# Cosine-similarity attention on one core: a third polynomial chunk, statistics instructions for Q, and one normalisation for two heads

## The chip, the cores and the metric

The kernel runs on one core of a Trainium2 chip. A core has five engines that matter here, each with an instruction queue of its own that is worked off strictly in order: TensorE (PE, matrix multiply; PEld is its weight load), VectorE (DVE), ScalarE (ACT), GpSimd (POOL) and SyncE (SP, which issues most DMAs). An instruction that waits for a semaphore holds everything behind it on its engine. The metric is the device time of one execution in microseconds; the kernel before has a median of 189.31 us over three runs (189.05 to 189.56).

## The reference, cut to what matters

```python
Q_norm = Q / (np.linalg.norm(Q, axis=-1, keepdims=True) + 1e-10)     # batch 8, heads 12, seq 512, dim 64
K_norm = K / (np.linalg.norm(K, axis=-1, keepdims=True) + 1e-10)
scores = np.einsum('bhqd,bhkd->bhqk', Q_norm, K_norm) / tau          # tau = 0.1
weights = np.exp(scores - np.max(scores, axis=-1, keepdims=True))
weights = weights / (np.sum(weights, axis=-1, keepdims=True) + 1e-10)
return np.einsum('bhqk,bhkd->bhqd', weights, V)
```

There are 96 heads. Each needs the norms of 512 rows of Q and of K, a 512 x 512 matrix of scores, 262,144 exponentials, and a product with V. Scores lie between -10 and 10, so the kernel leaves the maximum out.

## The kernel before, in words

**Tiling.** Two heads make a pair, 48 pairs in all, and a pair is one turn of a software pipeline. A pair's scores are made transposed, keys on the partitions: four chunks of 128 keys, each with 512 queries of both heads, so a chunk is a tile of 128 x 1024. Chunks alternate between two halves of a four-bank PSUM tile `scps`. The score of chunk n+2 can start when the exponential of chunk n has been read out, and that handover between TensorE and ScalarE is the innermost loop of the kernel.

**Stages of a pair.**

1. SP loads Q and K (tile `qk`, a ring of 15 pairs) and V (tile `vf`, a ring of 10).
2. GpSimd squares Q and K in one instruction (`sq`, line 366). TensorE adds the squares up with an identity matrix: 16 matmuls for Q and K together (line 396, pairs in `SUM_BOTH`), into a spare corner of the bank in which the output is summed. VectorE reduces the rest (line 410). Four pairs (35, 39, 43, 47, `BY_VECTOR`) are reduced by VectorE from the squares alone (line 418).
3. VectorE finds 1/norm for a group of one, two or four pairs at a time with a bit trick and two rounds of polynomial steps (lines 441 to 473, small tiles). The first three pairs use ScalarE's Ln and Exp for it.
4. Q is scaled by VectorE and K by VectorE or GpSimd (line 485; `K_ON_DVE` lists the pairs whose K goes to VectorE, 20 of 48).
5. TensorE transposes Q and K (line 494, 8 matmuls), VectorE evacuates the result (line 512, "the evacuation", tile `qt`).
6. TensorE makes the scores (line 633), ScalarE the exponentials (line 657, tile `et`).
7. GpSimd casts V to bf16 with a column of ones beside it (line 665, tile `vb`), so that the product also gives the sum of the weights. TensorE multiplies (line 682, 32 matmuls of 65 columns a pair) into two banks `oops`, one for each head.
8. VectorE takes the reciprocal of the sum (line 701) and multiplies (line 703), once for each head. SP stores the pair (line 707).

**Chunks that ScalarE does not do.** Chunk 3 of pairs 36 and 45 (`OFF`) gets its exponentials another way: scores go to the bank of the transposes (line 568), VectorE splits them into a power of two and a remainder (lines 573 and 575, for each head), and GpSimd evaluates a polynomial of the remainder in six steps (lines 596 to 604).

**What sets the order.** Nothing is decided at run time. Every operation is added to a list (`P.add`) with the operations it needs; `ORDER` then gives, for each engine, the written-out sequence of list numbers. `run` turns needs into semaphore waits. On each engine an operation thus waits for its own needs and for all that stands before it.

Of the kernel before, what the change touches and what calls it, by code (L numbers as in the profile page):

```python
# [108 lines left out]
def bass_cosine_similarity_attention_kernel(  # L109
# [70 lines left out]

    def key(name, s, *rest):
        return (name, s) + rest if s >= 0 else None
# [8 lines left out]
        vb[:, :, :, :, DIM : DIM + 1].rearrange("p r c h o -> p (r c h o)"), 1.0))  # L191
# [131 lines left out]
    def pair(s):  # L323
# [210 lines left out]
    def last_step(s, c):  # L534
        return 5 if (s, c) in OFF_ON_POOL + OFF_ON_BOTH else 4

# [17 lines left out]
    def poly(s, c, at):  # L554
# [4 lines left out]
        a0, a1, a2, a3, a4 = POLY_K if here else POLY  # L559
# [39 lines left out]
        if (s, c) in OFF_ON_POOL:  # L599
            k = cc ** 0.5  # L600
            steps = [("pool", "yt", mul(w, z, z)), ("pool", "ys", add(w, w, a1, k)),
                     ("pool", "ys", lambda e: e.tensor_scalar(out=z, in0=z, scalar1=a2 * cc, scalar2=a3 * cc, op0=ALU.mult, op1=ALU.add)),
                     ("pool", "yt", mul(w, w, w)), ("pool", "yt2", lambda e: e.tensor_tensor(out=w, in0=w, in1=z, op=ALU.add)),
                     ("pool", "yt3", mul(e_, w, p2))]
        elif (s, c) in OFF_ON_BOTH:
# [13 lines left out]
    def rest(s):  # L619
# [41 lines left out]
        def cast(e):  # L661
            out = vb[:, iq, :, :, 0:DIM].rearrange("p c h d -> p h c d")
            in_ = vf[iv][:, :, :].rearrange("p h (c d) -> p h c d", c=NT)
            if not in_psum(s):
                return e.tensor_scalar(out=out, in0=in_, scalar1=1.0, scalar2=1.0, op0=ALU.mult, op1=ALU.mult)  # L665
            assert s + R_QK >= NP and off_of[s] == NT - 1
            e.tensor_scalar(out=out[:, :, 0 : NT - 1], in0=in_[:, :, 0 : NT - 1], scalar1=1.0, scalar2=1.0, op0=ALU.mult, op1=ALU.mult)
            e.memset(vb[:, iq, NT - 1, :, DIM : DIM + 1].rearrange("p h o -> p (h o)"), KAPPA)
            return e.tensor_scalar(out=out[:, :, NT - 1], in0=in_[:, :, NT - 1], scalar1=KAPPA, scalar2=1.0, op0=ALU.mult, op1=ALU.mult)

        P.add(("VC", s), "pool", "vck" if in_psum(s) else "vc", T0 + 3.0 - slack(s, M_VC), [("LV", s), key("PV", s - R_QK, 0, NT - 1), key("PV", s - R_QK, 1, NT - 1), "vone"], cast)
# [3 lines left out]
        for h in range(2):  # L675
            for i in range(NT):
                def pv(e, h=h, i=i):
                    for c in range(NT):
                        t = i
                        if s in off_of:  # L680
# [28 lines left out]
    def last(s, T0):  # L709
        iq, iet, io = s % R_QK, s % R_ET, s % R_O  # L710
        spare = t_ps[:, :, :, :].rearrange("p w t x -> p (w t x)").bitcast(f32)
        for k, (h, lo, hi) in enumerate(PIECES):
            bank = spare if k == 2 else o_ps[h]
            order = [c for c in range(NT - 1) if c != off_of.get(s)] + [off_of[i] for i in (s,) if i in off_of] + [NT - 1]
            for j, c in enumerate(order):
                def pv(e, h=h, lo=lo, hi=hi, c=c, bank=bank, j=j):
                    for t in range(lo, hi):
                        at = 65 * (t - lo)
                        last = e.matmul(
                            out=bank[:, at : at + 65], lhsT=et[iet][:, c, h, 128 * t : 128 * t + 128],  # L720
                            rhs=vb[:, iq, c, h, :], start=(j == 0 and t == lo), stop=(j == NT - 1), skip_group_check=True)
# [3 lines left out]
                           [("EXP", s, c, k) if c == NT - 1 else exps(s, c)[0], ("VC", s)]  # L725
# [25 lines left out]
POLY = (-186.9751803485176, 100772.4799431421, -50373599.073513225, 207520169.07623482, 3.565140779347853e-11)  # L751
OFF = {(36, 3): (36, 36), (45, 3): (45, 45)}
# [14 lines left out]
STATS_FROM = 99  # L767
# [42 lines left out]
def slack(s, most):  # L810
# [129 lines left out]
```

## Time and profile before

| | us |
|---|---|
| median of three runs | 189.31 (189.05 to 189.56) |
| span of the profiled execution, first to last instruction | 186.8 |
| ScalarE busy | 180.2 |
| TensorE busy | 179.5 |
| GpSimd busy | 165.7 |
| VectorE busy | 159.9 |

The profile describes one execution, whose span is 186.8 us; what lies around the span (2.5 us up to the median) is not in it. A row of a group of instructions gives source line, engine, operation, the tiles written and read, their shapes, the count, busy time, mean duration in ns, and the idle time ahead of them with its releaser. A row of a timeline gives start, length, engine, line and a count where equal instructions were merged. Instructions of one engine overlap: the next starts before the last has drained, so the distance between two starts is what an instruction costs its engine, and its duration is longer. Lateness that is shorter than this overlap is not printed as idle time.

### The profile page before, as it was taken

How to read it: one execution, taken by the hardware profiler on the slowest of the kernel's cores; microseconds unless marked ns; L12 is line 12 of the kernel's file. 1: busy time of each engine (PE TensorE's matmuls, PEld its weight loads, DVE VectorE, ACT ScalarE, POOL GpSimd, SP SyncE). 2: the span in 40 equal slices, each digit the busy share in tenths (PEclk: the TensorE clock that was granted, in tenths of full speed). 3: DMA queues.
4: the chain of work that ended last, by engine and by line, in shares of the span. 5: the costliest groups of instructions: out<-in, count | busy, mean ns of one | idle time of the engine just before them, and what ended most of it. 6: DMA issues, size and time to landing. Idle time of an engine off the chain costs nothing.

```text
span 186.8 us, 7242 instructions
## 1 busy us (share of the span) xinstructions
PE 179.5 (96%) x3010; PEld 117.9 (63%) x3010; DVE 159.9 (86%) x523; ACT 180.2 (96%) x210; POOL 165.7 (89%) x147
## 2 busy tenths in 40 slices
PE   7889999999999999999999999999999999998993
PEld 2456766666667666666676666766656566555653
DVE  2789998987987978979889988999999999998664
ACT  5799999999999999999999999999999999999992
POOL 3799999999989998999999899999999999907940
PEclk9999999999999999999999999999999999999999
DMA  5999999999999877999999999999798731113135
GB/s 158 354 349 351 349 358 329 288 351 364 370 376 369 283 245 230 309 303 307 312 379 367 328 371 335 319 312 298 241 303 294 239 105 56 60 56 116 60 112 168
DMA packets 52447, 50.79 MB, mean 272 GB/s; under 512 B 3136, under 2 KB 52416, under 8 KB 52416
## 3 DMA queue, kind: packets, MB, share of 16 engines
q1 hardware_dynamic: 51984, 50.02, 81.8%
q8 instruction: 23, 0.38, 0.8%
q10 hardware_dynamic: 432, 0.33, 0.5%
q14 instruction: 8, 0.07, 0.1%
HBM read 37.75 MB, written 12.58 MB: 269 GB/s over the span
## 4 chain that ended last, share of the span: by engine, by line
ACT 92%; PE 3%; DVE 2%; DMA 1%; POOL 0%; issue 0%; DVEq 0%
ACT et L657 91%; DMA qk<-in_K_dram 1%; PE oops L682 1%; PE scps L633 1%; DVE xs L260 1%; DVE ob L732 0%; POOL sq L256 0%; PE tps L283 0%; ACT ys L432 0%; DVE qn L273 0%; DVE ob L703 0%; PE oops L401 0%; ACT nps L435 0%; PE oops L281 0%; DVE rd L730 0%
## 5 line engine op out<-in xcount | busy, mean ns | idle before, releaser
L657 ACT ACTIVATE et<-scps 128x1024 bf16<-128x1024 f32 (+1 forms) x191 | 173.8, 1155 | 0.3 <-PE scps L633 0.3
L366 POOL TENSOR_TENSOR sq<-qk 128x1024 bf16<-128x1024 f32 x44 | 82.8, 1895 | 0.6 <-DMA qk<-in_K_dram 0.6
L633 PE MATMUL scps<-qt 64*128 64x512 bf16 x380 | 74.5, 386 | 2.2 <-ACT et L657 1.0
L682 PE MATMUL oops<-vb,et 128*128 128x65 bf16 x1504 | 75.8, 194 | 0.1
L682 PEld LDWEIGHTS oops<-vb,et 128*128 128x128 bf16 x1504 | 57.0, 98 | 27.7 <-issue 21.9
L485 DVE TENSOR_TENSOR qn<-qk,nps 128x512 bf16<-128x512 f32 x67 | 44.2, 678 | 0.7 <-ACT nps L435 0.6
L703 DVE TENSOR_TENSOR ob<-oops,rd 128x256 f32<-128x256 f32 x94 | 39.5, 422 | 1.7 <-DVE ys L447 0.2
L512 DVE COPY qt<-tps 128x1024 bf16<-128x1024 bf16 x47 | 32.3, 687 | 3.9 <-PE tps L494 3.0
L494 PE MATMUL tps<-ident,qn 128*128 128x128 bf16 x376 | 34.3, 220 | 0.6 <-DVE qn L485 0.6
L485 POOL TENSOR_TENSOR qn<-qk,rk 128x512 bf16<-128x512 f32 x27 | 28.1, 1045 | 2.6 <-DVE rk L443 1.7
L665 POOL TENSOR_SCALAR vb<-vf 128x512 bf16<-128x512 f32 x48 | 29.3, 629 | 0.2
L633 PEld LDWEIGHTS scps<-qt 64*128 64x128 bf16 x380 | 18.3, 92 | 16.5 <-ACT et L657 4.8
L396 PE MATMUL oops<-sq,ident 128*128 128x64 bf16 x640 | 27.6, 192 | 0.0
L494 PEld LDWEIGHTS tps<-ident,qn 128*128 128x128 bf16 x376 | 21.7, 98 | 9.4 <-issue 3.4
L396 PEld LDWEIGHTS oops<-sq,ident 128*128 128x128 bf16 x640 | 22.2, 97 | 6.1 <-issue 5.7
L701 DVE RECIPROCAL rd<-oops 128x4 f32<-128x4 f32 x94 | 16.5, 178 | 10.4 <-PE oops L682 5.2
L410 DVE TENSOR_REDUCE nps<-oops 128x16 f32<-128x64 f32 x40 | 8.7, 217 | 2.0 <-PE oops L396 2.0
L596 POOL TENSOR_TENSOR xw<-xz 128x1024 f32<-128x1024 f32 x2 | 3.8, 1895 | 5.6 <-DVE xz L575 5.6
L443 DVE SCALAR_TENSOR_TENSOR nps<-nps,ys 128x32 f32<-128x32 f32 (+3 forms) x45 | 7.9, 190 | 0.4
L195 PE MATMUL oops<-warm_in 128*128 128x512 bf16 x10 | 4.4, 631 | 1.0 <-DVE warm_in L199 1.0
L357 POOL TENSOR_TENSOR sq<-qk 128x512 bf16<-128x512 f32 (+1 forms) x5 | 4.6, 954 | 0.8 <-DMA qk<-in_K_dram 0.6
L418 DVE TENSOR_REDUCE nps<-sq 128x8 f32<-128x512 bf16 x8 | 5.3, 684 | 0.0
(64 smaller groups left out, 72.5 us busy)
## 6 DMA issues: line engine op xcount, KB each, us to landing
vf<-in_V_dram SPq DMA_DIRECT2D x48, 256.0 KB, 5.6
qk<-in_Q_dram SPq DMA_DIRECT2D x47, 256.0 KB, 4.4
qk<-in_K_dram SPq DMA_DIRECT2D x47, 256.0 KB, 5.8
out_dram<-ob SPq DMA_DIRECT2D x47, 256.0 KB, 3.8
qk<-in_Q_dram SPq DMA_DIRECT2D x2, 128.0 KB, 2.6
qk<-in_K_dram ACTq DMA_DIRECT2D x2, 128.0 KB, 2.8
out_dram<-ob SPq DMA_DIRECT2D x1, 128.0 KB, 1.9
out_dram<-ob SPq DMA_DIRECT2D x1, 64.0 KB, 1.8
```

The lines of the kernel that those rows point to most:

```text
L366: lambda e: e.tensor_tensor(out=sqf, in0=data, in1=data, op=ALU.mult))
L396: last = e.matmul(out=o_ps[bank][:, 320:384], lhsT=ident[:, :], rhs=sq[iqs][:, :, 4 * k : 4 * k + 4], start=(k == 0), stop=(k == 15), skip ...
L410: lambda e, bank=bank, dst=x2[:, :, c8 : c8 + 8]: e.tensor_reduce(out=dst, in_=o_ps[bank][:, 320:384].rearrange("p (w g e) -> p w g e", w= ...
L485: lambda e, w=w, r=r: e.tensor_tensor(out=qn[iqn][:, w].rearrange("p t h d -> p h t d"), in0=qk[iq][:, w].rearrange("p h (t d) -> p h t d" ...
L494: last = e.transpose(t_ps[:, w, t, :], qn[iqn][:, w, t].rearrange("p h d -> p (h d)"), ident[:, :])
L512: lambda e, ws=ws: e.tensor_copy(out=qt[iqt][:, ws, :, :].rearrange("p w t x -> p (w t x)"), in_=t_ps[:, ws, :, :].rearrange("p w t x -> p ...
L633: last = e.matmul(out=sc_ps[:, 2 * b + h, :], lhsT=qt[iqt][64 * h : 64 * h + 64, 1, c, :], rhs=qt[iqt][64 * h : 64 * h + 64, 0, :, :], sta ...
L657: lambda e, c=c, b=b, hs=hs: e.activation(out=et[iet][:, c, hs[0] : hs[-1] + 1, :], in_=sc_ps[:, 2 * b + hs[0] : 2 * b + hs[-1] + 1, :], f ...
L665: return e.tensor_scalar(out=out, in0=in_, scalar1=1.0, scalar2=1.0, op0=ALU.mult, op1=ALU.mult)
L682: last = e.matmul(out=o_ps[h][:, 65 * t : 65 * t + 65], lhsT=et[iet][:, c, h, 128 * t : 128 * t + 128], rhs=vb[:, iq, c, h, :], start=(i = ...
L701: lambda e, hs=slice(0, 2) if s in RCPJ else hs, grid=r_all: e.reciprocal(out=rd[io][:, hs, :], in_=grid[:, :, :, DIM]))
L703: lambda e, hs=hs, grid=grid: e.tensor_tensor(out=ob[io][:, hs], in0=grid[:, :, :, 0:DIM], in1=rd[io][:, hs, :].unsqueeze(3).to_broadcast( ...
```

## The change

- **Third chunk.** `OFF` gets chunk 3 of pair 27. All three chunks use a polynomial of lower degree: five steps on GpSimd where there were six (the step at line 603 goes).
- **Statistics for Q of 36 pairs.** For the groups in `STATS` (pairs 12 to 47) the squares of Q are not made. VectorE runs four statistics instructions (`bn_stats`) a pair on Q itself, each over two rows read alternately, element by element, 256 bytes apart in SBUF. Three more small steps a group turn mean and deviation into the sum of squares. GpSimd squares K alone, and TensorE adds with 8 matmuls instead of 16. Pairs 4 to 11 keep the 16. `BY_VECTOR` is empty: the pairs that were reduced from squares by VectorE go through TensorE as well.
- **Joint products.** For pairs 4 to 46, without 27, 36 and 45, one reciprocal and one multiplication serve both heads. They wait for the last product of both, and both output banks come free together.
- **Keys.** `K_ON_DVE` falls to pairs 1 to 4: sixteen key scalings move from VectorE to GpSimd.
- **V.** From pair 4 on, GpSimd casts V of two pairs in one instruction, when both have been loaded; `vb` has 14 pairs in its ring instead of 15 and another layout.
- **Loads.** Q and K of a ring place have a semaphore each.
- **Orders.** The sequences of all engines are written anew from about pair 4 on. In the first pairs a few neighbours change places.

```diff
-    R_QK, R_V, R_SQ, R_QN, R_QT, R_ET, R_O, R_X = RINGS
+    R_QK, R_V, R_SQ, R_QN, R_QT, R_ET, R_O, R_X, R_VB = RINGS
...
-    vf = [sb(f"vf{i}", [128, 2, NT * DIM], f32) for i in range(R_V)]
-    vb = sb("vb", [128, R_QK, NT, 2, DIM + 1], bf16)
+    vf = sb("vf", [128, R_V, 2 * NT * DIM], f32)
+    vb = sb("vb", [128, R_VB, 2, NT, DIM + 1], bf16)
...
+    def cast_of(s):
+        return ("VC", s - 1 if s - 1 in CAST_TWO else s) if s >= 0 else None
...
     def stats(s):
-        return s >= STATS_FROM and group[s] not in NORM_ON_ACT
+        return group[s] in STATS
...
-                  slot=f"first{s}_{w}" if s <= 3 else f"qk{iq}")
+                  slot=f"first{s}_{w}" if s <= 3 else f"qk{iq}_{w}")
...
         if (s, c) in OFF_ON_POOL:
-            k = cc ** 0.5
-            steps = [("pool", "yt", mul(w, z, z)), ("pool", "ys", add(w, w, a1, k)),
-                     ("pool", "ys", lambda e: e.tensor_scalar(out=z, in0=z, scalar1=a2 * cc, scalar2=a3 * cc, op0=ALU.mult, op1=ALU.add)),
-                     ("pool", "yt", mul(w, w, w)), ("pool", "yt2", lambda e: e.tensor_tensor(out=w, in0=w, in1=z, op=ALU.add)),
-                     ("pool", "yt3", mul(e_, w, p2))]
+            steps = [("pool", "yt", mul(w, z, z)), ("pool", "ys", add(w, w, a1, cc)),
+                     ("pool", "ys", lambda e: e.tensor_scalar(out=z, in0=z, scalar1=a2, scalar2=1.0, op0=ALU.add, op1=ALU.mult)),
+                     ("pool", "yt", mul(w, w, z)), ("pool", "yt3", mul(e_, w, p2))]
...
+        if cast_of(s)[1] == s:
+            n = 2 if s + 1 < NP and cast_of(s + 1)[1] == s else 1
+            ib = s % R_VB
+
+            def cast(e):
+                return e.tensor_scalar(
+                    out=vb[:, ib : ib + n, :, :, 0:DIM].rearrange("p r h c d -> p (r h c) d"),
+                    in0=vf[:, iv : iv + n, :].rearrange("p r (x d) -> p (r x) d", d=DIM), scalar1=1.0, scalar2=1.0, op0=ALU.mult, op1=ALU.mult)
+
+            P.add(("VC", s), "pool", "vc" if n == 1 else "vc2", T0 + 3.0 - slack(s, M_VC),
+                  [("LV", s + i) for i in range(n)] + [key("PV", s + i - R_VB, h, NT - 1) for i in range(n) for h in range(2)] + ["vone"], cast)
...
-OFF = {(36, 3): (36, 36), (45, 3): (45, 45)}
+OFF = {(27, 3): (27, 27), (36, 3): (36, 36), (45, 3): (45, 45)}
+CAST_TWO = (4, 6, 8, 10, 12, 14, 16, 18, 20, 22, 24, 26, 28, 30, 32, 34, 36, 38, 40, 42, 44, 46)
-BY_VECTOR = (35, 39, 43, 47)
+BY_VECTOR = ()
-SUM_BOTH = (4, 5, 6, 7, 8, 9, 10, 11, 12, 13, 14, 15, 16, 17, 18, 19, 20, 21, 22, 23, 24, 25, 26, 27, 28, 29, 30, 31, 32, 33, 34, 36, 37, 38, 40, 41, 42, 44, 45, 46)
+SUM_BOTH = (4, 5, 6, 7, 8, 9, 10, 11)
-STATS_FROM = 99
+STATS = (8, 9, 10, 11, 12, 13, 14, 15, 16, 17, 18)
-JOINT = False
+JOINT = True
-JOINT_FROM = 0
-OFF_ON_POOL = ((36, 3), (45, 3))
+JOINT_FROM = 4
+OFF_ON_POOL = ((27, 3), (36, 3), (45, 3))
-K_ON_DVE = (1, 2, 3, 4, 9, 12, 15, 18, 21, 24, 27, 30, 33, 36, 39, 40, 42, 44, 46, 47)
+K_ON_DVE = (1, 2, 3, 4)
-RINGS = 15, 10, 6, 4, 4, 4, 8, 3
+RINGS = 15, 10, 6, 4, 4, 4, 8, 3, 14
...
 ORDER = {
```

The statistics themselves stood in the code before, unused (lines 378 to 387 and 459 to 467):

```python
for h in range(2):
    rows = qk[iq][:, 0, h, :].rearrange("p (t d) -> p t d", t=NT)
    for t in range(0, NT, 2):
        last = e.bn_stats(out=st[:, g % R_X, c8 + 4 * h + t : c8 + 4 * h + t + 2, :].rearrange("p g x -> p (g x)"),
                          in_=rows[:, t : t + 2].rearrange("p t d -> p d t"))
```

More of the change, by code (lines that the diff above doesn't have):

```diff
@@ L534, in last_step @@
     def last_step(s, c):
[L535 removed]
+        return 4
     def exps(s, c):
@@ L558, in poly @@
         here = in_psum(s)
-        a0, a1, a2, a3, a4 = POLY_K if here else POLY
+        a0, a1, a2, a4 = POLY
         lift = LIFT_K if here else LIFT
@@ L659, in rest @@
                           func=ACT.Exp, scale=math.log(2.0) / UNIT if s in off_of else inv_tau))
[L661 to L671, printed above, removed]
+        if cast_of(s)[1] == s:
[7 more added lines that the diff above has]
+                  [("LV", s + i) for i in range(n)] + [key("PV", s + i - R_VB, h, NT - 1) for i in range(n) for h in range(2)] + ["vone"], cast)
         if last_pair:
@@ L720, in pv @@
                             out=bank[:, at : at + 65], lhsT=et[iet][:, c, h, 128 * t : 128 * t + 128],
-                            rhs=vb[:, iq, c, h, :], start=(j == 0 and t == lo), stop=(j == NT - 1), skip_group_check=True)
+                            rhs=vb[:, s % R_VB, h, c, :], start=(j == 0 and t == lo), stop=(j == NT - 1), skip_group_check=True)
                     return last
                 op = P.add(("PV", s, k, c), "pe", "pv" if hi - lo == NT else "pvh", T0 + 0.9 * c + 2.5 + 0.1 * k,
-                           [("EXP", s, c, k) if c == NT - 1 else exps(s, c)[0], ("VC", s)]
+                           [("EXP", s, c, k) if c == NT - 1 else exps(s, c)[0], cast_of(s)]
                            + ((evas(last_eva) + [freed(*u) for i in range(last_eva, NP) for u in turn_user.get(i, [])[-1:]] if k == 2 else bank_free[s, h]) if c == order[0] else [("PV", s, k, order[j - 1])]), pv)
```

14 lines of the change are left out of this document (7 added, 7 removed), and 158 rows, old and new, of the table ORDER.

## The prediction

> **What bounds the kernel now.** I read the page's engine list first, then the chain that ended last, then the timelines of single engines, because the list alone cannot separate four engines that are all above 85%.
>
> ```profile
> span 186.8 us, 7242 instructions
> PE 179.5 (96%) x3010; PEld 117.9 (63%) x3010; DVE 159.9 (86%) x523; ACT 180.2 (96%) x210; POOL 165.7 (89%) x147
> ACT 92%; PE 3%; DVE 2%; DMA 1%; POOL 0%; issue 0%; DVEq 0%
> 11.89 167.82 ACT et L657 x183
> ```
>
> The chain is ScalarE's exponentials from 11.89 us to 179.71 us without a break: 183 of them in 167.82 us, 0.917 us each. The timeline of ScalarE shows that 0.917 is not the pure rate:
>
> ```profile
> 98.77 2.97 ACT L657 ACTIVATE et<-scps 128x1024 bf16<-128x1024 f32 x3
> 100.72 1.02 ACT L657 ACTIVATE et<-scps 128x1024 bf16<-128x1024 f32 x1
> 120.83 13.95 ACT L657 ACTIVATE et<-scps 128x1024 bf16<-128x1024 f32 x15
> 134.40 3.14 ACT L657 ACTIVATE et<-scps 128x1024 bf16<-128x1024 f32 x3
> ```
>
> From 120.83 to 134.40 fifteen start 0.905 us apart; from 98.77 to 100.72 two steps take 1.95 us, 0.14 too much. Successive exponentials overlap, so no idle time is printed for it. In all, 167.82 - 183 x 0.905 = 2.2 us are lost to scores that come late. TensorE's timeline tells why:
>
> ```profile
> 88.04 0.39 PE L633 MATMUL scps<-qt 64*128 64x512 bf16 x2
> 88.36 0.79 PE L682 MATMUL oops<-vb,et 128*128 128x65 bf16 x20
> 89.08 0.39 PE L633 MATMUL scps<-qt 64*128 64x512 bf16 x2
> ...
> 99.14 0.39 PE L633 MATMUL scps<-qt 64*128 64x512 bf16 x2
> 99.47 0.42 PE L682 MATMUL oops<-vb,et 128*128 128x65 bf16 x8
> 99.72 0.63 PE L396 MATMUL oops<-sq,ident 128*128 128x64 bf16 x16
> 100.28 0.39 PE L633 MATMUL scps<-qt 64*128 64x512 bf16 x2
> ...
> 103.46 0.61 PE L494 MATMUL tps<-ident,qn 128*128 128x128 bf16 x8
> 104.00 0.39 PE L633 MATMUL scps<-qt 64*128 64x512 bf16 x2
> ```
>
> A pair of scores blocks TensorE 0.32 us; 20 products take 0.72 (0.036 each), 16 sums of squares 0.56 (0.035), 8 transposes 0.54. One pair of heads (a "turn", four exponentials, 3.62 us) needs 4 x 0.32 + 32 x 0.036 + 0.54 + 0.56 = 3.53 us of TensorE. So TensorE is nearly full too, and a stretch between two scores with over 0.9 us of work (1.04 and 1.14 us here) delays an exponential.
>
> **The change, part by part.** Times are laid against this execution's span, 186.8 us; the median 189.31 is 2.5 us more, which I keep.
>
> *Third chunk off ScalarE.* One exponential less: -0.905 us on the chain. Its cost lies elsewhere:
>
> ```profile
> L573 DVE TENSOR_SCALAR xp<-tps 128x512 int16<-128x512 f32 x4 | 2.7, 682 | 0.0
> L596 POOL TENSOR_TENSOR xw<-xz 128x1024 f32<-128x1024 f32 x2 | 3.8, 1895 | 5.6 <-DVE xz L575 5.6
> L595 POOL TENSOR_SCALAR xw<-xw 128x1024 f32<-128x1024 f32 x2 | 2.1, 1045 | 0.2
> L603 POOL TENSOR_TENSOR xw<-xw,xz 128x1024 f32<-128x1024 f32 x2 | 4.7, 2354 | 0.2
> L596 POOL TENSOR_TENSOR et<-xw,xp 128x1024 bf16<-128x1024 f32 x2 | 4.3, 2130 | 0.2
> L366 POOL TENSOR_TENSOR sq<-qk 128x1024 bf16<-128x1024 f32 x44 | 82.8, 1895 | 0.6 <-DMA qk<-in_K_dram 0.6
> L357 POOL TENSOR_TENSOR sq<-qk 128x512 bf16<-128x512 f32 x4 | 4.0, 1039 | 0.1
> L485 POOL TENSOR_TENSOR qn<-qk,rk 128x512 bf16<-128x512 f32 x27 | 28.1, 1045 | 2.6 <-DVE rk L443 1.7 <-DVE nps L443 0.7 <-PE tps L494 0.2
> L665 POOL TENSOR_SCALAR vb<-vf 128x512 bf16<-128x512 f32 x48 | 29.3, 629 | 0.2
> ```
>
> VectorE gets four more steps of 512 elements. GpSimd's chain of a chunk is 2 x 1.895 + 2 x 1.045 + 2.354 + 2.130 = 10.4 us now; without the 2.354 step it is 8.0. Three chunks cost 24.0 where two cost 20.7: +3.3. The new chain (pair 27) ends some 9 us after its last step on VectorE, one key scaling in between, and the products that read it stand about 1.5 us later: hidden.
>
> *GpSimd.* Squares of 36 pairs shrink from 1.895 to 1.039: -30.8. Sixteen key scalings come over from VectorE at 1.045: +16.7. The 22 double casts lie between 1.045 (L595, as many elements) and 2 x 0.629; I take 1.15, nearer the plain pass: 44 x 0.629 - 22 x 1.15 = -2.4 (bounds -4.7 and 0). With the chunk's +3.3: 165.7 - 13.2 = 152.5 us. No time on the chain, since GpSimd releases nothing there now; the extra room covers the moved scalings, whose transposes otherwise wait. The cast needs two loads of V instead of one; V has a ring of ten pairs, so the second is there. SP's queue is reordered too: the last loads of pairs 46 and 47 now stand behind the stores of pairs 26 to 33.
>
> ```profile
> qk<-in_Q_dram SPq DMA_DIRECT2D x47, 256.0 KB, 4.4
> ```
>
> Store 33 can go in turn 35 to 36; 4.4 us, 1.2 turns, after it Q of pair 47 has landed, and its statistics stand in turn 38: nothing.
>
> *TensorE.* Pairs 12 to 47 lose 8 of 16 sums: -36 x 0.28 = -10 us, and a turn falls to 3.25 of 3.62. Counting the orders' stretches over 1.02 us, I find 31 before and 25 after. At 2.2/31 = 0.07 us each that is -0.4. One new stretch is bad: behind score 4.3 stand 20 products and 16 sums, 0.32 + 0.72 + 0.56 = 1.60 us; a score must start 0.44 before its exponential (100.28 to 100.72), so 1.60 - 0.905 - 0.46 = +0.23. Net -0.2; bounds -1 (most of the lateness goes) and +0.5.
>
> *VectorE.* Here the change adds. The costs per instruction are distances between starts, not durations:
>
> ```profile
> 62.46 0.23 DVE L410 TENSOR_REDUCE nps<-oops 128x16 f32<-128x64 f32 x1
> 62.61 0.19 DVE L443 SCALAR_TENSOR_TENSOR nps<-nps,ts 128x32 f32<-128x32 f32 x1
> 62.70 0.17 DVE L701 RECIPROCAL rd<-oops 128x4 f32<-128x4 f32 x1
> 62.83 0.18 DVE L443 SCALAR_TENSOR_TENSOR nps<-nps,ys 128x16 f32<-128x16 f32 x1
> 62.92 0.42 DVE L703 TENSOR_TENSOR ob<-oops,rd 128x256 f32<-128x256 f32 x1
> 63.25 0.68 DVE L485 TENSOR_TENSOR qn<-qk,nps 128x512 bf16<-128x512 f32 x1
> 63.85 0.17 DVE L443 SCALAR_TENSOR_TENSOR rk<-nps,ys 128x16 f32<-128x16 f32 x1
> ...
> 69.70 0.68 DVE L512 COPY qt<-tps 128x1024 bf16<-128x1024 bf16 x1
> 70.30 0.25 DVE L443 SCALAR_TENSOR_TENSOR nps<-nps,ys 128x16 f32<-128x16 f32 x2
> ```
>
> Reduction 0.15, reciprocal 0.13, product with 256 elements 0.33, scaling with 512 elements 0.60, small step 0.09, evacuation 0.60. A joint product (512 elements) is then 0.60 for 0.66, and one reciprocal of two goes. The statistics instruction (128 elements, four a pair) has no row. By the slope between 256 and 512 elements, 1.05 ns each, it is 0.33 - 0.135 = 0.195; bounds are 0.15 (64 elements) and 0.33 (256). I take 0.195. The fullest stretch lies between the evacuations of pairs 9 and 22, 13 turns or 13 x 3.62 = 47.0 us. The new order has there 13 evacuations (7.8), 14 scalings (8.4), 13 joint products (7.8), 13 reciprocals (1.7), 16 reductions (2.4), 61 small steps (5.5): 33.6, and 64 statistics (12.5): 46.1, or 98%. (Before: 13, 18, 26 halves, 26, 16, 51: 7.8 + 10.8 + 8.6 + 3.4 + 2.4 + 4.6 = 37.6.) It fits with 0.9 us to spare, so I cost it at nothing; the cover is that queries' evacuations run about 1 us before the scores that need them. From 22 to 35: 32.0 + 52 x 0.195 = 42.1 of 46.2.
>
> [...]
>
> *Joint products.* Both banks of a pair now come free together, so the next pair's first product waits for one reciprocal and one product of 512 elements: 0.22 (62.70 to 62.92) + about 0.69, 0.9 us after the last matmul. The orders leave one to two scores between, 0.9 to 1.8 us. Behind that wait on TensorE stand the next scores. I cost it at nothing, covered by the 0.37 us of slack a turn; bounds 0 and +3 (rival below). At the end pair 46's joint product sits before the last pair's products: +0.1.
>
> Sum: 186.8 - 0.9 - 0.2 + 0.1 = 185.8; with 2.5: **188.3 us**. Own range, with TensorE's bounds: 187.5 to 189.0.
>
> **Rivals.**
> 1. *VectorE becomes the bound between pairs 9 and 22.* Decides from (47.0 - 33.6)/64 = 0.209 us for a statistics instruction, only 0.014 above my value. At 0.25: 33.6 + 16.0 = 49.6, +2.6 us: 190.9. At 0.27 +3.9: 192.2. For it: 98% already. Against it: the 0.60 rows show few ns beyond element count.
> 2. *Statistics read at half rate* (256 elements' worth, 0.33): 33.6 + 21.1 - 47.0 = +7.7, and from 22 to 35 32.0 + 17.2 - 46.2 = +3.0: 199.0. Against it: TensorE's sums (L396) read pieces of 8 bytes, 128 bytes apart, at 0.035 each, no slower than the products at 0.036; but that is another engine. [...]
> 3. *Banks freed late.* If the joint product comes behind a statistics group (0.78 us) or an evacuation, TensorE waits. Up to 0.37 us a turn is free; at 0.45, 33 turns lose 0.08 each: 2.6 us, 190.9.
> 4. *No gain, because TensorE, not ScalarE, sets the pace:* the scores of the third chunk stay on TensorE, and lateness rises by what ScalarE saves: 189.2. Against it: the 0.905 run at 120.83.
>
> **How the numbers follow.** Differences under 0.3% (0.57 us) cannot be told from none. Forecast 0.55 (0.47 faster, 0.07 same, 0.01 slower); rival 4 0.08 (same); rival 1 0.18, rival 3 0.11, rival 2 0.08 (slower). Faster 0.47, same 0.15, slower 0.38. The range goes from 187.5 to 192.3, rival 1 at 0.27; rival 2, the far ends of 1 and 3, and a gain over 1.8 us stay outside.
>
> **What would show it.** Right: exponentials still 0.905 to 0.92 apart with one fewer; VectorE 90 to 96% busy in 35 to 85 us with few waits of TensorE for it; statistics instructions 0.19 to 0.20 apart; TensorE's groups of 16 sums gone after pair 12; GpSimd near 152 us. Wrong: exponentials over 0.93 apart between 35 and 85 us with scores waiting for an evacuation (rival 1 or 2, told apart by the distance of the statistics); products waiting for L703 (rival 3); lateness of 3 us spread evenly (rival 4).

## The result, and the profile after

The changed kernel takes 189.63 us (median of 22 runs) where the kernel before takes 189.05 us (22 runs on the same chips): a ratio of 1.0028, 95% interval 1.0015 to 1.0041. Two of the 22 runs were slow (192.4 and 192.5 us, at granted clocks of 0.987 and 0.989 where the other 20 had 0.990 to 1.000); they, and one run each of e3, e11 and e14 below, stand in the medians and not in the ratios. Forecast were 188.3 us, 1.0 us less than the 189.31 known then; measured is 0.5 to 0.6 us more. The profiled spans say the same: 186.8 us before and 187.4 us after.

From the page of the changed kernel, the span, the busy times and the chain that ended last:

```profile
span 187.4 us, 6908 instructions
PE 175.9 (94%) x2786; PEld 112.3 (60%) x2786; DVE 167.1 (89%) x594; ACT 179.6 (96%) x209; POOL 152.2 (81%) x144
ACT 52%; PE 20%; POOL 11%; DVE 10%; DMA 3%; POOLq 1%; issue 1%; SPq 1%; DVEq 0%
```

TensorE and GpSimd have less to do, as intended (179.5 to 175.9 and 165.7 to 152.2 us), and VectorE more (159.9 to 167.1). But the chain that was 92% ScalarE is 52% ScalarE now, and 20% of it is TensorE. The pieces of this chain in order of time (start, length, what), with two long runs of exponentials and what stands between and behind them:

```profile
27.92 60.61 ACT et L658 x66
...
104.96 0.59 DVE xz L578
...
105.84 2.04 POOL qn L488 x2
107.88 1.89 POOL xw L599
...
112.09 1.04 POOL qn L488
...
115.53 2.14 POOL et L599
117.71 0.30 PE oops L683 x4
...
125.38 36.78 ACT et L658 x40
```

Before, one run of 183 exponentials reached from 11.89 to 179.71. Now the chain is off ScalarE ahead of 27.92, from 88.53 to 125.38 (the polynomial of pair 27, up to 117.71, is a part of it) and from 162.16 to the end.

**An account by distance.** Successive exponentials of 1024 columns start 0.904 us apart at the median of both profiled runs, and never under 0.903. For each distance between the starts of two exponentials I take what it has above 0.904 us, and call the sum of this from pair 2 to chunk 2 of pair 47 the lateness. (Chunk 3 of pair 47 is divided and counted with what follows it.) "5.0" is chunk 0 of pair 5. Lateness in us by turns:

| turns | 2-6 | 7-11 | 12-16 | 17-21 | 22-26 | 27-31 | 32-36 | 37-41 | 42-46 | 47 | all |
|---|---|---|---|---|---|---|---|---|---|---|---|
| before | 0.17 | 0.25 | 0.19 | 0.18 | 0.55 | 0.10 | 0.18 | 0.25 | 0.24 | 0.01 | 2.12 |
| after | 0.77 | 0.12 | 0.22 | 0.39 | 0.17 | 0.73 | 0.09 | 0.39 | 0.07 | 0.50 | 3.44 |

One exponential less is -0.90, the lateness +1.32, the divided last chunk and what follows it +0.19, the start -0.02: +0.59, the difference of the spans. So the question is where 1.32 us of lateness come from. It rises in three stretches, by 0.60 (turns 2 to 6), 0.63 (27 to 31) and 0.49 (turn 47); in all the others together it falls by 0.40. 2.1 us of the 3.44 stand in eight places: 5.0 (0.54), 17.0 (0.20), 30.0 (0.22), 31.3 (0.27), 39.0 and 41.2 (0.18 each), 47.1 and 47.2 (0.35 and 0.15). In nearly all later runs these return within 0.04 us where no edit touched them.

The terms of the sum that can be read at once, from the groups of the changed kernel:

```profile
L386 DVE BATCH_NORM_STATS2 st<-qk 128x6 f32<-128x128 f32 x144 | 31.4, 281 | 0.0
L704 DVE TENSOR_TENSOR ob<-oops,rd 128x512 f32<-128x512 f32 (+1 forms) x54 | 33.3, 618 | 0.4
L667 POOL TENSOR_SCALAR vb<-vf 128x1024 bf16<-128x1024 f32 (+1 forms) x26 | 25.4, 981 | 0.3
L599 POOL TENSOR_TENSOR xw<-xz 128x1024 f32<-128x1024 f32 x3 | 5.7, 1893 | 3.3 <-DVE xz L578 3.3
L599 POOL TENSOR_TENSOR xw<-xw,xz 128x1024 f32<-128x1024 f32 x3 | 7.1, 2357 | 0.2
L599 POOL TENSOR_TENSOR et<-xw,xp 128x1024 bf16<-128x1024 f32 x3 | 6.4, 2130 | 0.2
```

and from the waits of the changed kernel (waiter, releaser: us in total, times, longest):

```profile
PEld oops L683 <- DVE ob L704: 3.7, 16, 0.3
PEld oops L683 <- POOL et L599: 1.6, 3, 0.7
```

The window 35 to 85 us, where VectorE was forecast to be fullest, of the kernel before and then of the changed one (stretch, length; busy time and instructions of PE, PEld, DVE, ACT, POOL; granted clock, DMA share, GB/s):

```profile
35.00:85.00 50.00, 49.96 (x894) 34.18 (x894) 42.74 (x155) 50.00 (x56) 48.22 (x40) 1.00 0.97 318
```

```profile
35.00:85.00 50.00, 48.45 (x779) 31.28 (x778) 48.21 (x199) 50.00 (x56) 40.31 (x40) 1.00 0.98 325
```

VectorE is 96.4% busy there, TensorE's longest wait for a product on VectorE is 0.3 us, and there are 56 exponentials in both. VectorE is not the bound.

### The profile page after: what moved, and what is told of

It is laid out like the page before. It is cut to its first block, busy times and chain, and to the rows that moved or that the text cites. A ratio compares the mean times of both kernels' runs of the same rounds, so it can differ in the third digit from the quotient of the medians.

```text
span 187.4 us, 6908 instructions
## 1 busy us (share of the span) xinstructions
PE 175.9 (94%) x2786; PEld 112.3 (60%) x2786; DVE 167.1 (89%) x594; ACT 179.6 (96%) x209; POOL 152.2 (81%) x144
## 4 chain that ended last, share of the span: by engine, by line
ACT 52%; PE 20%; POOL 11%; DVE 10%; DMA 3%; POOLq 1%; issue 1%; SPq 1%; DVEq 0%
ACT et L658 52%; PE oops L683 8%; PE scps L634 7%; POOL xw L599 5%; DMA qk<-in_Q_dram 3%; PE tps L497 3%; DVE qt L515 2%; DVE ob L704 2%; POOL qn L488 2%; PE oops L399 1%; DVE st L386 1%; POOLq L87 1%; DVE qn L488 1%; POOL et L599 1%; POOL xw L598 1%; POOL xz L604 1%
## 5 line engine op out<-in xcount | busy, mean ns | idle before, releaser
L488 POOL TENSOR_TENSOR qn<-qk,rk 128x512 bf16<-128x512 f32 x43 | 44.3, 1042 | 14.7 <-DVE rk L446 14.7
L366 POOL TENSOR_TENSOR sq<-qk 128x512 bf16<-128x512 f32 x36 | 37.0, 1039 | 3.3 <-DMA qk<-in_K_dram 3.2
L488 DVE TENSOR_TENSOR qn<-qk,nps 128x512 bf16<-128x512 f32 x51 | 33.9, 677 | 0.7 <-ACT nps L438 0.7
L704 DVE TENSOR_TENSOR ob<-oops,rd 128x512 f32<-128x512 f32 (+1 forms) x54 | 33.3, 618 | 0.4
L515 DVE COPY qt<-tps 128x1024 bf16<-128x1024 bf16 x47 | 32.1, 682 | 1.6 <-PE tps L497 1.3
L386 DVE BATCH_NORM_STATS2 st<-qk 128x6 f32<-128x128 f32 x144 | 31.4, 281 | 0.0
L667 POOL TENSOR_SCALAR vb<-vf 128x1024 bf16<-128x1024 f32 (+1 forms) x26 | 25.4, 981 | 0.3
L404 PE MATMUL oops<-sq,ident 128*128 128x64 bf16 x336 | 16.8, 193 | 0.7 <-POOL sq L360 0.6
L702 DVE RECIPROCAL rd<-oops 128x8 f32<-128x8 f32 (+1 forms) x54 | 10.6, 197 | 6.9 <-PE oops L683 5.6
L369 POOL TENSOR_TENSOR sq<-qk 128x1024 bf16<-128x1024 f32 x8 | 15.1, 1892 | 0.2 <-DMA qk<-in_K_dram 0.2
L404 PEld LDWEIGHTS oops<-sq,ident 128*128 128x128 bf16 x336 | 12.5, 98 | 4.0 <-issue 2.2
```

What stands on the lines that cost most here:

```text
L366: lambda e: e.tensor_tensor(out=sqf[:, 8 * DIM :], in0=data[:, 8 * DIM :], in1=data[:, 8 * DIM :], op=ALU.mult))
L386: last = e.bn_stats(out=st[:, g % R_X, c8 + 4 * h + t : c8 + 4 * h + t + 2, :].rearrange("p g x -> p (g x)"), in_=rows[:, t : t + 2].rearr ...
L404: last = e.matmul(out=o_ps[bank][:, at : at + 64], lhsT=ident[:, :], rhs=sq[iqs][:, 8 * w : 8 * w + 8, 8 * k : 8 * k + 8], start=(k == 0), ...
L488: lambda e, w=w, r=r: e.tensor_tensor(out=qn[iqn][:, w].rearrange("p t h d -> p h t d"), in0=qk[iq][:, w].rearrange("p h (t d) -> p h t d" ...
L515: lambda e, ws=ws: e.tensor_copy(out=qt[iqt][:, ws, :, :].rearrange("p w t x -> p (w t x)"), in_=t_ps[:, ws, :, :].rearrange("p w t x -> p ...
L667: return e.tensor_scalar(out=vb[:, ib : ib + n, :, :, 0:DIM].rearrange("p r h c d -> p (r h c) d"), in0=vf[:, iv : iv + n, :].rearrange("p ...
```

## The experiments

All times stand beside runs of the kernel before on the same chip in the same hour (its medians were 188.9 to 189.1). "Late" is the lateness of the profiled run.

| | median us (runs) | ratio to before, 95% | span | late |
|---|---|---|---|---|
| changed kernel | 189.63 (22) | 1.0028 [1.0015, 1.0041] | 187.4 | 3.44 |
| e1_sums_back | 189.73 (7) | 1.0042 [1.0023, 1.0060] | 188.1 | 3.89 |
| e2_wait27_moved | 189.40 (9) | 1.0030 [1.0015, 1.0045] | 187.1 | 3.21 |
| e3_end_as_before | 189.34 (12) | 1.0026 [1.0008, 1.0043] | 187.9 | 3.22 |
| e4_three_edits | 189.07 (11) | 1.0000 [0.9986, 1.0014] | 187.3 | 3.07 |
| e5_first_turns | 192.09 (4) | 1.0169 [1.0153, 1.0186] | 190.2 | 5.85 |
| e6_two_chunks | 191.44 (5) | 1.0130 [1.0115, 1.0144] | 189.1 | 4.39 |
| e7_halves | 189.41 (12) | 1.0029 [1.0006, 1.0051] | 187.5 | 3.67 |
| e8_rows_in_a_line | 189.3 (1) | | 187.3 | 3.45 |
| e9_load_wait | 189.34 (12) | 1.0021 [1.0006, 1.0035] | 187.4 | 3.00 |
| e10_turns_4_to_9 | 193.31 (6) | 1.0247 [1.0222, 1.0272] | 192.7 | 7.18 |
| e11_all_spread | 195.09 (6) | 1.0315 [1.0285, 1.0344] | 193.1 | 6.94 |
| e12_two_chunks_again | 190.91 (5) | 1.0102 [1.0087, 1.0117] | 190.2 | 4.08 |
| e13_fewer_sums | 189.12 (12) | 1.0017 [0.9992, 1.0043] | 187.3 | 3.01 |
| e14_two_spread | 189.42 (12) | 1.0017 [0.9988, 1.0045] | 187.5 | 3.10 |
| e15_two_chunks_halves | 190.14 (7) | 1.0073 [1.0046, 1.0099] | 188.1 | 3.17 |

In the diffs, a line of TensorE's order is what stands between two scores: "5.0:" is the stretch behind score 5.0, "P27.1.3" a product of pair 27, head 1, part 3 (4 matmuls; for a polynomial pair part 3 is the polynomial chunk), "S8" sums (8 matmuls, two of them for pairs up to 11), "T31" a transpose (4).

### Three places relieved

```diff
 e1, TensorE
-4.3: P3.1.0 P3.1.1 P3.1.2 P3.0.3 P3.1.3 S8 S8 | 5.0:
+4.3: P3.1.0 P3.1.1 P3.1.2 P3.0.3 P3.1.3 | 5.0: S8 S8
```

> The changed kernel with one edit in TensorE's order: the 16 sums of pair 8, which stand between score 4.3 and score 5.0 behind 20 products, go behind score 5.0. Theory A (placement): the third chunk does take 0.9 us off ScalarE, and single overfull places of the new order give it back; exponential 5.0, 0.54 us late in the changed kernel, is then at most 0.1 late, and the time falls by 0.4 to 0.5 us, to 1.000 of the kernel before (0.999 to 1.001). Theory B (congestion): TensorE and VectorE are full on the whole, so lateness taken away in one place comes back in the next; exponential 5.0 is on time but the time stays within 0.15 us of the changed kernel (1.002 to 1.004).

TensorE between scores 4.3 and 5.0 in the changed kernel (start, length, what, count):

```profile
25.91 0.39 PE L634 MATMUL scps<-qt 64*128 64x512 bf16 x2
26.23 0.85 PE L683 MATMUL oops<-vb,et 128*128 128x65 bf16 x20
26.93 0.63 PE L399 MATMUL oops<-sq,ident 128*128 128x64 bf16 x16
27.49 0.61 PE L634 MATMUL scps<-qt 64*128 64x512 bf16 x4
```

The two scores are 1.58 us apart, as forecast (1.60), and exponential 5.0 follows late. Exponentials of the changed kernel and then of e1:

```profile
23.66 3.85 ACT L658 ACTIVATE et<-scps 128x1024 bf16<-128x1024 f32 x4
27.92 5.61 ACT L658 ACTIVATE et<-scps 128x1024 bf16<-128x1024 f32 x6 [0.41 <-PE scps L634]
```

```profile
23.83 5.69 ACT L658 ACTIVATE et<-scps 128x1024 bf16<-128x1024 f32 x6
29.78 3.86 ACT L658 ACTIVATE et<-scps 128x1024 bf16<-128x1024 f32 x4 [0.26 <-PE scps L634]
```

5.0 is on time in e1, but 5.2 is 0.37 us late and 6.0 0.10: turns 2 to 6 keep 0.79 us of lateness, and the time stays where theory B had it. The place alone did not make it. (The profiled run of e1 is also 0.50 us late at 8.2; e3 shows what that is.)

```diff
 e2, TensorE
-29.3: P27.0.3 S35 P27.1.1 | 30.0: P27.1.2 T31 P27.1.3
+29.3: P27.1.1 P27.1.2 P27.0.3 S35 | 30.0: T31 P27.1.3
```

> The changed kernel with one edit in TensorE's order: the product of pair 27 that reads the polynomial chunk, and the eight sums behind it, go two products later. Theory A: TensorE's wait for GpSimd's last step of pair 27 (0.28 us before the product at 117.71) shrinks to under 0.1, exponentials 30.0 and 31.3 (0.22 and 0.27 late) lose some 0.3 together, the time falls by 0.2 to 0.4 us (1.001 of before). Theory B: no change of more than 0.1 us (1.003).

In the changed kernel TensorE waits for pair 27's polynomial:

```profile
117.71 0.30 PE L683 MATMUL oops<-vb,et 128*128 128x65 bf16 x4 [0.28 <-POOL et L599]
```

In e2 the wait is gone and turns 27 to 31 fall from 0.73 to 0.49; 30.0 keeps 0.10 of its 0.22. The median falls by 0.2 us, which its interval cannot tell from nothing.

```diff
 e3: pair 46 in two halves, TensorE's and VectorE's end as before
-46.3: P45.1.0 P45.0.0 P45.1.1 P45.1.2 | 47.0: P45.1.3 P45.0.1 P45.0.2 | 47.1: P45.0.3 P46.1.0 P46.1.1 P46.1.2
+46.3: P45.0.0 P45.0.1 P45.0.2 P45.1.0 | 47.0: P45.1.1 P45.1.2 | 47.1: P45.0.3 P45.1.3
```

> The changed kernel with its end put as in the kernel before: pair 46 gets two reciprocals and two products again instead of joint ones, and TensorE's and VectorE's order from score 46.3 on is that of before, so that the products which read pair 45's polynomial chunk stand behind score 47.1. Theory A: exponentials 47.1 and 47.2 (0.35 and 0.15 late) are on time, and the first product of pair 47 no longer waits 0.54 us for the joint product; the time falls by 0.5 to 0.7 us, to 0.999 to 1.000 of before. Theory B: GpSimd's chain of pair 45 ends too late wherever the products stand, and at most 0.2 us is won (1.002).

The end of the changed kernel, on TensorE:

```profile
179.62 0.54 PE L683 MATMUL oops<-vb,et 128*128 128x65 bf16 x12 [0.43 <-POOL et L599]
...
183.30 0.67 PE L720 MATMUL oops<-vb,et 128*128 128x65 bf16 x16 [0.54 <-DVE ob L704]
```

A polynomial is waited for again (pair 45), and then the joint product of pair 46 holds the last pair's products. In e3 both waits and the 0.50 us of turn 47 are gone. The time does not show it: the ratio is 1.0026 where theory A had 0.999 to 1.000. The profiled run had another late place, 0.45 us at 8.2, because VectorE waited for a load:

```profile
37.50 0.89 DVE L386 BATCH_NORM_STATS2 st<-qk 128x6 f32<-128x128 f32 x4 [1.09 <-DMA qk<-in_Q_dram]
```

The statistics are the first readers of a Q, and what stands behind them on VectorE was held with them: the next joint product started at 39.35 us in e3 and at 38.61 in the changed kernel, the next evacuation at 40.16 and 39.41. The late load is that of pair 12's Q, which stands behind two stores in SP's queue. In the profiled run of the changed kernel it lands at 36.23 us, the statistics start at 36.25, and no wait is printed. In e1, e3, e4 and e12 VectorE waits 0.9 to 1.1 us for it, and 8.2 is 0.28 to 0.50 us late. From the start of the last chunk (47.3) to the end e3's run took 5.4 us, and e4's with the same end 4.9, so spans alone do not tell half a microsecond; the lateness does.

> The three edits together (sums of pair 8 behind score 5.0; the waiting product of pair 27 later; the end as before). Theory A: the gains add up to 1.1 to 1.5 us, time 0.995 to 0.997 of the kernel before, that is, faster than both kernels. Theory B: less than 0.5 us, 1.000 to 1.003 of before.

e4, all three edits: the time of the kernel before (ratio 1.0000, where theory A had 0.995 to 0.997). About half a microsecond is won back, no more. Its profiled run is late at 5.2 (0.38 us) as e1 is, and at 8.2 (0.36) for the load.

### The full turns

```diff
 e9, VectorE (besides e4's edits): the statistics of pair 12 later
-evacuation 8, statistics 12, small steps of group 7, evacuation 9
+evacuation 8, small steps of group 7, statistics 12, evacuation 9
```

> The three edits of e4_three_edits, and in VectorE's order the statistics of pair 12 stand one evacuation later (ahead of evacuation 9 instead of behind evacuation 8), so that a late Q load of pair 12 holds up less. If single places make the lateness: the 0.36 us at exponential 8.2 go, the lateness is 2.7 us and the median 188.7. If TensorE's sum of work sets the pace, the 0.36 turns up within the next turns, the lateness stays 3.0 to 3.2 and the median 189.0 to 189.1.

8.2 is on time, and 9.1 and 10.2 are late instead (0.18 and 0.10 us): turns 7 to 11 have 0.47 us as in e4. The lateness moved, as the rival said, but not for its reason. Ahead of score 9.1 TensorE is idle, because its transposes wait for a scaling that now stands behind the moved statistics on VectorE:

```profile
42.91 0.62 PE L497 MATMUL tps<-ident,qn 128*128 128x128 bf16 x8 [0.36 <-DVE qn L488]
```

And e14 below, which has e4's edits and a shorter wait for the same load (0.35 us), has 0.11 us in turns 7 to 11. So the 0.36 us at 8.2 in e4 were the load's, and not TensorE's sum of work.

```diff
 e13, TensorE's sums
-for k in range(8 * w, 8 * w + 8):
+for k in [k for k in range(8 * w, 8 * w + 8) if not 6 <= s <= 9 or k == 0 or k % 2]:
```

> The changed kernel without 28 of its sum matmuls (7 of the 16 of each of the pairs 6 to 9, so that their statistics are incomplete and the output is not the reference's); every order and every wait stays. They take about 7 x 0.035 = 0.25 us of TensorE in each of four turns, 1.0 us in all. If TensorE's sum of work makes the 0.77 us of lateness in turns 2 to 6, 0.5 us or more of it go and stay gone: lateness 2.9, median 189.1. If another engine's wait makes it, the lateness stays 3.4 and the median 189.5.

Exponentials of e13 in the same stretch of time as above:

```profile
23.96 9.42 ACT L658 ACTIVATE et<-scps 128x1024 bf16<-128x1024 f32 x10
```

Turns 2 to 6 fall from 0.77 to 0.34 us, 5.0 from 0.54 to 0.20, and turns 7 to 11 stay at 0.11. (The median is 189.12 us as the first theory had it, but the intervals of the two ratios overlap.) Nothing but TensorE's work was changed, so in turns 2 to 6 TensorE's work makes the lateness.

It is not the total of that work, since the kernel before has 16 sums for the same pairs and only 0.17 us of lateness here. It is how the new order deals it out. The table counts TensorE's matmuls in the traces, from a pair's first score to the next pair's, and prices them as the prediction does (0.16 us a score, 0.036 a product, 0.035 a sum, 0.0675 a transpose). ScalarE needs 3.62 us a turn (4 x 0.905).

| TensorE's work, us, in turn | 2 | 3 | 4 | 5 | 6 |
|---|---|---|---|---|---|
| before | 3.68 | 3.68 | 3.53 | 3.66 | 3.54 |
| changed kernel | 3.52 | 3.68 | 4.24 | 3.53 | 3.53 |
| e1 | 3.52 | 3.68 | 3.68 | 4.09 | 3.53 |
| e13 | 3.52 | 3.43 | 3.75 | 3.29 | 3.53 |

The changed kernel has 32 sums and 36 products in turn 4, and its late place is 5.0, right behind it. The kernel before, too, has a turn with 32 sums, turn 5, but only 20 products in it. e1 carries the excess over to turn 5, and the lateness follows to 5.2 and 6.0.

```diff
 e5, e10: TensorE up to score 9.0 in the order of the kernel before (a pair's last products later), VectorE fitted to it;
 e5 with joint products from pair 8 only, e10 with all
```

> The changed kernel with its first turns put back: TensorE's order up to score 9.0 and VectorE's up to the evacuation of pair 8 are those of the kernel before, joint products start at pair 8 instead of 4, and the first statistics (pair 12) stand behind pair 6's products on VectorE instead of ahead of them, those of pairs 13 and 14 behind evacuation 10. Theory A2 (TensorE's queue is overfull in turns 2 to 6, where pairs still need 16 sums, and the statistics of pair 12 can wait on VectorE for a load): lateness of the exponentials of turns 2 to 6 falls from 0.77 us to under 0.3, none is over 0.2 us late in turns 7 to 11, and the time falls by 0.4 to 0.7 us, 0.999 to 1.000 of before. Theory B (lateness moves on): under 0.15 us, 1.002.

> TensorE's order up to score 9.0 as in the kernel before, VectorE's order of the same turns fitted to it with the joint products kept, the statistics of pair 12 behind pair 6's joint product and evacuation 9, and the edits for pair 27 and for the end as in e4_three_edits. TensorE has 3.6 us of work in each of the turns 4 to 9 and as much time, so some lateness there must stay. If single places make it: turns 2 to 11 are 0.45 us late as in the kernel before instead of 1.3 in e4_three_edits, the lateness is 2.3 and the median 188.3. If TensorE's sum sets the pace: turns 2 to 11 stay at 0.9 or more, and the median is 189.0.

Both are worse. In e5, whose TensorE has the work of the kernel before in turns 2 to 6, these turns came down to 0.44 us; but it has statistics pushed into turns 10 and 11, which VectorE could not hold there (2.9 us late in turns 7 to 11), so its time tells little. e10 shows what the joint products ask of the order. TensorE and then VectorE near 8.2, which is 1.93 us late:

```profile
42.12 0.56 PE L683 MATMUL oops<-vb,et 128*128 128x65 bf16 x12
44.15 0.37 PE L683 MATMUL oops<-vb,et 128*128 128x65 bf16 x4 [1.48 <-DVE ob L704]
```

```profile
42.58 0.68 DVE L515 COPY qt<-tps 128x1024 bf16<-128x1024 bf16 x1
43.18 0.20 DVE L702 RECIPROCAL rd<-oops 128x8 f32<-128x8 f32 x1
43.41 0.69 DVE L704 TENSOR_TENSOR ob<-oops,rd 128x512 f32<-128x512 f32 x1
```

The next pair's first product stands right behind the last of this pair, and needs an evacuation, a reciprocal and the whole joint product to be over. In halves, its bank could have been free while the other head's products ran; e15 below shows that for pair 27.

### The third chunk alone

```diff
-OFF = {(27, 3): (27, 27), (36, 3): (36, 36), (45, 3): (45, 45)}
+OFF = {(36, 3): (36, 36), (45, 3): (45, 45)}
 e6: pair 27's joint product among the small steps of group 15; e12: ahead of them; e15: pair 27 in two halves
```

> The changed kernel with the third chunk given back to ScalarE (pair 27 like its neighbours, joint products included), all else kept. If the third chunk were worth its 0.9 us whole, this would be 0.9 us slower than the changed kernel (1.0075 of before). Theory A2: the chunk's wait on TensorE (exponentials 30.0 and 31.3) goes with it, some 0.4 us, so it is 0.4 to 0.6 us slower than the changed kernel, 1.005 to 1.006. Theory C (the third chunk is worth nothing, since TensorE still makes its scores): equal to the changed kernel, 1.0025 to 1.0035.

> The changed kernel with chunk 27 on ScalarE again, as e6_two_chunks, but the joint product of pair 27 stands ahead of the small steps of group 15 on VectorE and not among them. If the 1.14 us at exponential 30.2 in e6_two_chunks came from that place in VectorE's order, they go: 190.2 to 190.4, 0.4 to 0.5% above the changed kernel, so that the third chunk is worth 0.6 to 0.9 us of its 0.905. If they came from the chunk itself, the median is 191.4 again.

> As e12_two_chunks_again, with pair 27 normalized in two halves as in the kernel before, so that the first bank is free before the second half's products end. If the 0.70 us at exponential 30.2 were the joint product's, they go, and what is left over the changed kernel is the third chunk: 190.2, 0.6 us above it if the chunk's own lateness costs 0.3, 190.5 if the chunk is worth its whole 0.905. If the chunk brings nothing, 189.6.

TensorE around the last products of pair 27 and the first of pair 28, in e12 and then in e15:

```profile
120.93 0.29 PE L683 MATMUL oops<-vb,et 128*128 128x65 bf16 x4
121.15 0.39 PE L634 MATMUL scps<-qt 64*128 64x512 bf16 x2
122.24 0.30 PE L683 MATMUL oops<-vb,et 128*128 128x65 bf16 x4 [0.70 <-DVE ob L704]
```

```profile
120.54 0.29 PE L683 MATMUL oops<-vb,et 128*128 128x65 bf16 x4
120.77 0.39 PE L634 MATMUL scps<-qt 64*128 64x512 bf16 x2
121.09 0.59 PE L683 MATMUL oops<-vb,et 128*128 128x65 bf16 x13
```

Exponential 30.2 is 1.14 us late in e6, 0.70 in e12 and on time in e15: it was the joint product, which without the chunk's own order stood too near to the next pair. e15 is the clean price: its span is 0.65 us above the changed kernel's (the time from the start of 47.3 is 4.8 us in both), its median 0.5 us, its ratio 0.45% (0.85 us; the intervals of both are 0.1 to 0.3% wide to each side). The third chunk is worth 0.5 to 0.85 of its 0.905 us; in the profiled runs it adds 0.27 of lateness. It was not the chunk that failed: without it, everything else together costs 1.2 us (188.1 to 186.8).

### Dense stretches after turn 12

```diff
 e11 (all four, on e10), e14 (the first two, on e4), TensorE
-16.2: T17 | 16.3: P15.0.0 P15.0.1 P15.0.2 P15.0.3 S23
+16.2: T17 P15.0.0 P15.0.1 | 16.3: P15.0.2 P15.0.3 S23
-31.2: P29.1.2 P29.0.2 P29.0.3 S37 P29.1.3 | 31.3: T33
+31.2: P29.0.2 P29.0.3 S37 | 31.3: P29.1.2 P29.1.3 T33
-33.1: P31.1.0 P31.1.1 S39 P31.1.2 P31.1.3 | 33.2: T35
+33.1: P31.1.0 S39 P31.1.1 | 33.2: P31.1.2 P31.1.3 T35
-41.1: P39.0.0 P39.0.1 P39.0.2 P39.0.3 S47 | 41.2: P39.1.0 P39.1.1
+41.1: P39.0.0 P39.0.1 P39.0.2 P39.0.3 | 41.2: S47 P39.1.0 P39.1.1
```

> As e10_turns_4_to_9, and at scores 17.0, 31.3, 33.2 and 41.2 the 24 matmuls that stand between two scores are divided: 8 of them go to the neighbouring stretch, which has 8. If single places make the lateness, 0.2 at 17.0, 0.2 at 31.3 and 0.19 at 41.2 go: the lateness is 1.7 us and the median 187.7, 0.7% under the kernel before, which would be the whole of the 0.9 us that the third chunk takes off ScalarE. If TensorE's sum sets the pace, the late places move by a turn and the median is 189.

> The three edits of e4_three_edits, and of the spreadings of e11_all_spread only the two that were gains there, at scores 17.0 and 31.3. If lateness after turn 12 is made at single places: 0.2 us at each go, the lateness is 2.65 and the median 188.65, 0.2% below the kernel before. If it moves on, 189.05 as e4_three_edits.

e11 carries e10's stalls, so only its later turns say something. 17.0 and 31.3 come on time in both. But in e14 16.3 is 0.30 us late, 32.1 0.27 and 33.2 0.26. From turn 12 to turn 36 the lateness is 1.29 us in e4 and 1.71 in e14, so the two edits cost 0.4 us; the sums (3.07 and 3.10) hide this, since e4's run has 0.36 at 8.2 for the load. Two of the new late places have a wait, on TensorE of e14 ahead of 16.3 (first products of pair 15) and of 32.1 (first products of pair 30):

```profile
70.24 0.43 PE L683 MATMUL oops<-vb,et 128*128 128x65 bf16 x8 [0.21 <-DVE ob L704]
...
126.30 0.43 PE L683 MATMUL oops<-vb,et 128*128 128x65 bf16 x8 [0.15 <-DVE ob L704]
```

Pair 15's first products now come before the joint product of pair 14 is over. Pair 29's products end later, so its joint product does, and pair 30 waits for it. Why 33.2 is late was not shown. Whether another division of the stretches would do better stays open; none that was tried was faster than the kernel before.

### VectorE's two new operations

```diff
 e7
-JOINT = True
+JOINT = False
 e8
-in_=rows[:, t : t + 2].rearrange("p t d -> p d t")
+in_=rows[:, t : t + 2].rearrange("p t d -> p (t d)")
```

> The changed kernel without joint products: two reciprocals and two products a pair at the places of the joint ones. Theory A2 with VectorE at its limit (46.1 of 47.0 us between evacuations 9 and 22, statistics at 0.196): 13 times 0.19 us more make 48.6, so lateness between pairs 9 and 22 rises by 1 to 2 us, time 1.007 to 1.013 of before. Theory D (the wait for both heads costs more than it saves): TensorE's waits for L704 (3.7 us in the changed kernel) go under 2 and the time falls, 0.999 to 1.002.

> The changed kernel with the statistics instruction reading its 128 elements one after another instead of two rows alternately, 256 bytes apart. The sums of squares of Q come out wrongly grouped, so the output is not the reference's; the count of elements and all else is the same. If distance in SBUF costs VectorE, the distance between two statistics falls from 0.196 us towards 0.15; if not, it stays at 0.19 to 0.20.

e7, with all products in halves in the changed kernel's orders: the time of the changed kernel, which neither theory had. VectorE, 97.9% busy from 35 to 85 us, still had room for the halves (its longest hold on a product of TensorE's is 0.4 us), and joint products by themselves bring nothing here (ratios 1.0028 with them, 1.0029 without). e8's group:

```profile
L386 DVE BATCH_NORM_STATS2 st<-qk 128x6 f32<-128x128 f32 x144 | 30.9, 278 | 0.0
```

281 ns with the stride, 278 without; the mean distance of two successive ones is 0.199 and 0.195 us. Reading two rows alternately cost VectorE 3 ns of an instruction's duration and 0.004 us of its distance.

## Why the prediction was wrong

**The step that failed is TensorE's.** "Net -0.2; bounds -1 (most of the lateness goes) and +0.5": the lateness rose by 1.32 us. Of this the waits for GpSimd and the end (below) make 0.7; the rest, 0.6 us net, stands on TensorE and is over the bound too.

- "1.60 - 0.905 - 0.46 = +0.23" is the term that was mis-sized: turns 2 to 6 rose by 0.60. The distance of the scores was right (1.58). But score 4.3 started only 0.57 us ahead of its exponential (25.91 to 26.48) where 5.0 had 0.43, so 0.14 of lead could be taken off and not 0.46: 1.58 - 0.904 - 0.14 = 0.54. The lead was gone because the whole of turn 4 is overfull. The prediction counted with 3.53 us of work in each such turn of 3.62; the new order puts 4.24 into turn 4 (e13: less of it, 0.43 us less lateness; e1: moved on, the same lateness).
- "At 2.2/31 = 0.07 us each that is -0.4" came out in size: all turns but 2 to 6, 27 to 31 and 47 have 0.40 us less. As a rule it is luck. It takes lateness as a count of long stretches times a mean, and in e14 two stretches made shorter were paid for in others, at 16.3 and 32.1 because a product waits for the joint product ahead of it (0.21 and 0.15 us).
- Turns 27 to 31 rose by 0.63, of which e2 puts 0.24 down to GpSimd. The other 0.4 us are not the third chunk's, since e15 has 0.52 us there without it (before: 0.10); half of that is at 31.3, behind 16 products and 8 sums in one stretch. Why this order has such stretches there stays open.

**The third chunk: price right, cover wrong.** e15 gives 0.5 to 0.85 us of the forecast 0.905. "Hidden" was wrong. The step that went is the plain square (1.893), not the 2.354 one, so a chain is 1.893 + 2 x 1.045 + 2.357 + 2.130 = 8.5 us, not 8.0; and at pair 27 it began behind two key scalings and held a third. VectorE's last step for it ended at 105.55 us (104.96 + 0.59) and GpSimd's at 117.67 (115.53 + 2.14): 12.1 us, where "some 9 us" with one scaling was forecast. Two more scalings are 2.1 of the difference, the step 0.5, GpSimd's wait for the scalings' factor 0.3. That is more than the margin of 1.5 us: TensorE waits 0.28 us for pair 27 (not the whole difference of 1.6, since TensorE itself reached that product 11.9 us after VectorE's last step and not 10.5) and 0.43 us for pair 45. e2 and e3 put the price of both, the joint product of pair 46 among it, at about 0.7 us of lateness (0.24 in turns 27 to 31, 0.50 in turn 47); e3 changes both waits at the end at once, so their shares were not told apart.

**The tail,** "+0.1": +0.19 with the divided last chunk, and 0.50 us ahead of it.

**VectorE: right.** Statistics 0.199 us apart where 0.195 was taken; 96.4% busy, just above the 90 to 96% forecast; joint products 0.60 us apart (0.598 to 0.609 for most). Rival 1 had a margin of 0.209 and did not come. Rival 2 (0.33 us each) did not come either: 0.199 us apart, and 281 ns long against 278 ns without the stride.

**GpSimd: right in sum, in part by luck** (152.2 us where 152.5 was forecast): 22 double casts at 1.05 us and not 1.15 are 2.2 us less, and three chains of 8.5 us and not 8.0 are 1.5 more.

**SP's queue, "nothing"**: the loads of pairs 46 and 47 did no harm, but Q of pair 12, which the prediction did not look at, holds VectorE up in some executions (0.9 to 1.1 us in e1, e3, e4 and e12).

**Joint products, "nothing": right in time (e7), wrong as a reason.** But for the last pair's (0.54 us at 183.30) no wait over 0.3 us is left in the changed kernel, because its orders keep a pair's products apart from the next pair's. Where an edit brought them nearer, rival 3's wait came at once: 1.48 us (e10), 0.70 (e12), 0.15 (e14). That this distance is also why the new orders have their dense stretches was not shown.

**The rivals.** Rival 4's time (189.2) came nearest, and so did its sign: lateness rises by more than ScalarE saves. Its mechanism, TensorE setting the pace, holds around turn 4. It is not the whole, and that its time came nearest is in part luck: the third chunk, which it has as worth nothing, is worth 0.5 us or more, and the lateness is not spread evenly but stands mostly in eight places, two of them (30.0 and 47.1) behind waits for GpSimd.

## What to carry to other kernels

When two engines are both about full, as ScalarE and TensorE were here (96% busy each), work taken off one is gained only as far as the other is on time: 0.90 us came off ScalarE, and the lateness of its exponentials rose by 1.32 us. So a forecast needs the second engine's work turn by turn in the new order, and not an average turn or the count of its long stretches: here one turn of 4.24 us in the place of 3.62 gave 0.5 us of lateness. A slack or margin of a hidden chain is to be counted with what stands ahead of it and inside it in its engine's order: two key scalings and 0.5 us of a wrongly named step used up a margin of 1.5 us here. The operation that serves two banks at once cost nothing by itself here (e7) but ties the order: in e12 the next pair's first product started 1.0 us after the last one had ended (121.22 to 122.24), 0.70 us of it idle, so an order with joint products has to put about as much other work between the two.

## What the runs showed of the hardware that was not expected

A statistics instruction over 128 elements takes 0.199 us when it reads two rows alternately, 256 bytes apart, and 0.195 us when it reads them in a line. A load that landed 0.02 us before it was needed in one execution (36.23 and 36.25 us) held VectorE for 1.09 us in another execution of nearly the same program (pair 12's Q, which landed 3.8 us after its issue in the changed kernel's profiled run and 4.9 us after it in e3's); a tail of such waits is not to be read from one profile.
